# First attention loads inside the last slot of conv pass one, and value products of 512 columns in two pieces

## The chip, the cores and the metric

One core of a Trainium2 chip runs the whole program. The metric is the device time of one execution in microseconds; lower is better.

The engines are named as in the profile: PE (TensorE, matmuls and transposes; PEld is its weight load), DVE (VectorE), ACT (ScalarE), POOL (GpSimd), and SP (SyncE, which issues most DMAs).

## The reference, cut to what matters

One layer of a streaming encoder for 2048 prompt rows and 32 sample rows of width 1024. One input projection feeds a convolution branch (h, B, C, z) and an attention branch (q, k, v, z_att) of 8 heads of 64 channels:

```
xn = rmsnorm(x, norm_in)
h, bg, cg, zc, q, k, v, za = project_in(xn, w_in)       # 8 x 512 columns
yc = bg * short_conv(cg * h, conv_w) * silu(zc)
ya = band_attention(q, k, v, rel, valid, rel_bias) * silu(za)
x  = x + concat(rmsnorm(yc, norm_conv), rmsnorm(ya, norm_att)) @ w_out
x  = x + sigmoid(rmsnorm(x, ple_norm) @ w_ple_gate) * (p @ w_ple_proj)
y  = rmsnorm(x, final_norm)
```

The newest keys and values and the last convolution rows are outputs too. `band_attention` lets each chunk of 64 queries see its own chunk and the 8 before it; the sample rows see 512 cached keys.

## The kernel before, in words

**Numbers.** Every product is taken in two parts: each operand is split into a high part in fp32r and a low part (the rest), and `products` (line 274) adds high x high, high x low and low x high, three matmuls per 128 rows of the contraction. With KT = 8 such steps a block of output takes 24 matmuls.

**Memory.** GR (fp32r) and GF (fp32) are two large tiles of SBUF, cut by hand into areas by offset. X, the normalized input, lies in GR for all five column chunks (`CHUNKS`: 256, 384, 512, 512 and 416 rows of tokens). Two weight sets `WS` (each a high and a low half of 8 x 256 columns) lie behind it, 4096 columns apart. Behind those is `O_SP`, 1536 free columns. The attention's areas lie over those of X: the keys `K` and values `V` over chunk 0 and the start of chunk 1, and the queries `Q` in two buffers, `O_Q = [9216, O_SP]`: group g uses buffer g % 2. Offset 9216 is the end of chunk 1. PSUM has eight banks; pass one takes banks 0 to 4 in turn (`psm`), and transposes banks 5 to 7.

**Order of the work.** The order of all instructions is written out by hand; each engine runs its own in that order, and semaphores hold an instruction until what it reads is written and what it overwrites is read. DMAs issued by SP leave in SP's order.

- Keys first (slots 0 and 1), while X is made. Then slots 2 to 7 (line 1021): two of queries (s = 2, 3), two of values (s = 4, 5), two of the attention's gate (s = 6, 7). A slot has 256 columns of weights, which `load_w` brings to RAW and `split_w` (ACT makes the high part, line 194, DVE the low part, line 195) splits into `WS[s % 2]`. In each slot the loop runs over the five chunks; behind chunk 1 it splits the weights of the next slot and loads those of the one after.
- `values` (line 341) works by tiles of 128 tokens: X is the stationary operand, the 256 weight columns (four heads) the moving one, so that a slot has 17 tiles of 24 matmuls of 256 columns. ACT copies the high part of a tile out of PSUM, DVE makes the low part, SP stores both to DRAM (`vd`, line 339). Tiles of the newest 512 rows and of the sample rows are also copied out plain (line 355) and stored as outputs.
- `background` (line 410) is called once per chunk: it splits two blocks of 128 x 512 of the later weights (ACT line 376, DVE 377), which SP stores to DRAM, and lets ACT issue the loads of the next two (line 371).
- Conv pass one (line 1130) computes the convolution branch for chunks 0 and 1 in eight slots u = 0 to 7, in pairs of (h, C) and (B, z). Each slot first stores its split weights to DRAM (`store_wc`), because passes two and three load them again (`load_wc`, line 1058, 2 MB). In the (B, z) slots the output of a chunk is made by DVE and POOL (line 1113) in one buffer T2, and stored by SP (line 1114). Behind u = 6 come the loads of the attention's biases, whose corners POOL masks (line 491).
- Behind pass one SP issues the first loads of the attention (lines 1144 to 1146): keys and queries of group 0, its values and gate, then keys and queries of group 1. A group is two heads by 256 queries. `load_kq` issues six DMAs (lines 447 and 454), `load_vz` two (lines 463 and 467).
- Then `dense` runs passes two and three of the convolution on PE (line 1096), and between its matmuls the attention is advanced piece by piece: scores (line 546), maximum on DVE, exponential on ACT, normalization on POOL (line 578), transposes (line 618), products with the values (line 664). The first scores are due after 3% of the dense columns.
- At the end the output projections run tile by tile.

Of the kernel before, what the change touches and what calls it, by code (L numbers as in the profile page):

```python
# [9 lines left out]
F32R = mybir.dt.float32r  # L10
AF = mybir.ActivationFunctionType
ALU = mybir.AluOpType
# [3 lines left out]
T = 2048  # L16
S = 32
# [4 lines left out]
KW = 512  # L22
# [4 lines left out]
KT = 8  # L27

C0 = T
S0 = T + KW  # L30
NKEY = T + KW + S
NKT = (NKEY + 127) // 128
CHUNKS = [(0, 256), (256, 384), (640, 512), (1152, 512), (1664, 416)]
NCH = len(CHUNKS)
# [4 lines left out]
O_WS = [2 * KT * TT, 2 * KT * TT + 4096]  # L39
O_SP = O_WS[1] + 4096  # L40
# [5 lines left out]
O_K = [0, 1536]  # L46
O_V = 3072
O_PT = [6144, 7680]
O_Q = [9216, O_SP]
O_Z = [O_SP + 1024, O_SP + 1280]  # L50

O_WO = XO[2]
# [11 lines left out]
def hybrid_encoder_kernel(  # L64
# [6 lines left out]
    act, dve, pool, pe, sp = nc.scalar, nc.vector, nc.gpsimd, nc.tensor, nc.sync  # L71
# [5 lines left out]
    vp = v_prompt[0, 0].rearrange("t h d -> t (h d)")  # L77
    ks = k_sample[0, 0].rearrange("t h d -> t (h d)")
    vs = v_sample[0, 0].rearrange("t h d -> t (h d)")
# [7 lines left out]
    vd = tc.dram_tile((NKT * 128, H, 2, HD), F32, name="vd")  # L87
# [18 lines left out]
    PS = pspool.tile([128, 8, 512], F32, name="PS")  # L106

    def R(off, *shape):
        n = 1
        for s in shape:  # L110
            n *= s
        v = GR[:, off:off + n]
        return v if len(shape) == 1 else v.rearrange("p (a b) -> p a b", a=shape[0])

    def G(off, *shape):
        n = 1
        for s in shape:
            n *= s
        v = GF[:, off:off + n]
        return v if len(shape) == 1 else v.rearrange("p (a b) -> p a b", a=shape[0])  # L120
# [27 lines left out]
    Xh = [R(XO[c], KT, n) for c, (_, n) in enumerate(CHUNKS)]  # L148
    Xl = [R(XO[c] + KT * n, KT, n) for c, (_, n) in enumerate(CHUNKS)]
# [13 lines left out]
    psm = Ring([0, 1, 2, 3, 4])  # L163
    pst = Ring([5, 6, 7])

    def cols(kind, i):
        return DC * "hBCzqkva".index(kind) + 128 * i
# [8 lines left out]
    def load_w(s):  # L176
        if s >= NS:
            return
        (k0, i0), (k1, i1) = slots[s]
        if k0 == k1:  # L180
            c = cols(k0, i0)
            sp.dma_start(RAW, win[:, c:c + 256].rearrange("(k p) n -> p k n", p=128))
        else:
            for j, (kk, ii) in enumerate(slots[s]):
                c = cols(kk, ii)
                sp.dma_start(RAW[:, :, j * 128:(j + 1) * 128],
                             win[:, c:c + 128].rearrange("(k p) n -> p k n", p=128))

    def split_w(s, ks_=range(KT)):
        if s >= NS:  # L190
            return
        wh, wl = WS[s % 2]
        for k in ks_:
            act.activation(wh[:, k], RAW[:, k], AF.Copy, scale=cT[:, k:k + 1])  # L194
            dve.scalar_tensor_tensor(wl[:, k], RAW[:, k], cT[:, k:k + 1],  # L195
                                     wh[:, k].bitcast(F32), ALU.mult, ALU.subtract)
# [77 lines left out]
    def products(out, wh, wl, xh, xl, ks_=range(KT), mid=None):  # L274

        for k in ks_:
            if mid and k == KT // 2:
                mid()
            pe.matmul(out, wh(k), xh(k), start=(k == ks_[0]), stop=False)  # L279
            pe.matmul(out, wh(k), xl(k), start=False, stop=False)  # L280
            pe.matmul(out, wl(k), xh(k), start=False, stop=(k == ks_[-1]))  # L281

    def block(s, j, c, bank=None, mid=None):
        wh, wl = WS[s % 2]
        ps = PS[:, psm() if bank is None else bank, 0:CHUNKS[c][1]]
        js = slice(j * 128, (j + 1) * 128)
        products(ps, lambda k: wh[:, k, js], lambda k: wl[:, k, js],
                 lambda k: Xh[c][:, k, :], lambda k: Xl[c][:, k, :], mid=mid)
        return ps
# [43 lines left out]
    def split_v(dst_r, src, rows, r0, h0):  # L333
        vhl = vhl_r().rearrange("p (h a d) -> p h a d", h=4, a=2)
        p4 = src.rearrange("p (h d) -> p h d", h=4)
        act.activation(vhl[rows, :, 0, :].bitcast(F32R), p4[rows], AF.Copy)
        dve.tensor_tensor(vhl[rows, :, 1, :].bitcast(F32R), p4[rows], vhl[rows, :, 0, :],
                          ALU.subtract)
        sp.dma_start(vd[r0:r0 + rows.stop - rows.start, h0:h0 + 4], vhl[rows])

    def values(s, c):
        wh, wl = WS[s % 2]
        h0 = 4 * (slots[s][0][1] // 2)
        t0, n = CHUNKS[c]
        for o in list(range(0, n - 127, 128)) + ([n - 128] if n % 128 else []):
            ps = PS[:, psm(), 0:256]
            products(ps, lambda k: Xh[c][:, k, o:o + 128], lambda k: Xl[c][:, k, o:o + 128],
                     lambda k: wh[:, k, :], lambda k: wl[:, k, :])
            p0 = 0 if o % 128 == 0 else 128 - S
            r0 = t0 + o if not p0 else S0  # L350
            rows = slice(p0, 128)
            split_v(None, ps, rows, r0, h0)
            if r0 >= T - KW:
                VR = VR_r()
                act.activation(VR[rows], ps[rows], AF.Copy)
                dst = vs if p0 else vp[r0 - (T - KW):r0 - (T - KW) + 128]
                sp.dma_start(dst[:, h0 * HD:(h0 + 4) * HD], VR[rows])
# [52 lines left out]
    def background():  # L410

        for work, LW in loaded:
            work(LW)
        del loaded[:]
        while todo and len(loaded) < 2:
            load, work = todo.pop(0)
            LW = LW_r()
            load(LW)
            loaded.append((work, LW))
# [18 lines left out]
    def load_kq(g):  # L438

        if g >= len(groups):  # L440
            return
        p, m = groups[g]
        t0, kn, qn = (256 * m, 256, 256) if m < 8 else (T, KW + S, S)
        k0 = t0 % (RING * 128)
        for h in range(2):
            rows = slice((2 * p + h) * HD, (2 * p + h + 1) * HD)
            sp.dma_start(K[h][:, k0:k0 + kn].bitcast(F32),
                         kd[:, rows, t0:t0 + kn].rearrange("b c t -> c b t"))
            for b in range(2):
                q = Q[g % 2][h][b]  # L450
                if m == 8:
                    pool.memset(q[:, 0:2 * S].bitcast(F32), 0.0)
                    q = q[:, h * S:(h + 1) * S]
                sp.dma_start(q[:, 0:qn].bitcast(F32),
                             qs[b, rows, t0:t0 + qn].unsqueeze(1).to_broadcast([HD, 2, qn]))

    def load_vz(g):
        if g >= len(groups):
            return
        p, m = groups[g]  # L460
        m0, m1 = (2 * m, 2 * m + 2) if m < 8 else (16, NKT)
        v0 = m0 % RING
        sp.dma_start(
            V[:, v0:v0 + m1 - m0, :].bitcast(F32),
            vd[m0 * 128:m1 * 128, 2 * p:2 * p + 2].rearrange("(m t) h a d -> t m (h a d)", t=128))
        t0, qn = 256 * m, 256 if m < 8 else S
        sp.dma_start(Z[g % 2][:, 0:qn], zd[p * 128:(p + 1) * 128, t0:t0 + qn])
# [537 lines left out]
    def spread(h):  # L1005
        sp.dma_start(ext2[h], ext[h].unsqueeze(0).to_broadcast([128, 768]))
# [13 lines left out]
    NP1 = 8  # L1020
    for s in range(2, NP1):
        kind = slots[s][0][0]
        for c, (t0, n) in enumerate(CHUNKS):
            if 3 <= s < 7 and c < 2:
                spread(2 * (s - 3) + c)
            if kind == "v":
                values(s, c)
            else:
                p0 = block(s, 0, c)
                p1 = block(s, 1, c)  # L1030
            if kind == "q":
                release()
                for j, ps in enumerate((p0, p1)):
                    split_store(ps, qs, slots[s][j][1], [(0, n, t0)], -0.125)
            elif kind == "a":
                for j, ps in enumerate((p0, p1)):
                    i = slots[s][j][1]
                    za = za_r()
                    act.activation(za[:, :n], ps, AF.Silu)
                    sp.dma_start(zd[i * 128:(i + 1) * 128, t0:t0 + n], za[:, :n])  # L1040
            if c == 1:
                split_w(s + 1)
                load_w(s + 2)
            background()
# [85 lines left out]
    for u in range(8):  # L1130
        s = NP1 + u
        store_wc(s)
        for i, _ in enumerate(conv(u, psm)):
            if i == KT:
                split_w(s + 1)
                load_w(s + 2)
        if u >= 6:
            load_wc(u + 2)
        if u == 6:
            load_bias(0)  # L1140
            load_bias8(0)
            mask_bias(0)

    load_kq(0)
    load_vz(0)
    load_kq(1)
    banks = Ring([6, 7])

# [74 lines left out]
```

## Time and profile before

| what | value |
|---|---|
| median of 3 runs | 1450.62 us (1447.92 to 1453.04) |
| profiled execution | 1452.03 us, span 1450.1 us |
| PE busy | 1421.2 us, 98% of the span |
| ACT, DVE, POOL busy | 542.3, 607.8, 317.4 us |
| mean granted PE clock | 0.993 |
| DMA | 249.10 MB, mean 172 GB/s |

The span runs from the first to the last instruction of the profiled execution. Busy times of PE are pipelined: a matmul's listed duration overlaps the next one's, so the pace is read from the starts of successive matmuls, not from durations. A wait is listed under the instruction that waited, with what released it. The chain of waits is followed back from the last instruction, and shows what each step waited for last.

### The profile page before, as it was taken

The numbers are of one execution on the slowest core, as the hardware profiler recorded it, in microseconds if no ns is written. First come the engines' busy times: TensorE is split into PE (matmuls) and PEld (weight loads), VectorE is DVE, ScalarE is ACT, GpSimd is POOL, SyncE is SP. The second block draws the span as 40 slices with busy tenths as digits, with TensorE's granted clock in tenths as the row PEclk, the third lists the DMA queues.
The fourth block names the chain that finished last, engine by engine and source line by source line (L and its number), as shares of the span: only waits on it lengthen the run. The fifth ranks groups of instructions, "written<-read, shape, count | busy, mean of one in ns | idle before, by whom it ended". The sixth has DMA issues, their size and how long they took to land.

```text
span 1450.1 us, 22728 instructions
## 1 busy us (share of the span) xinstructions
PE 1421.2 (98%) x8362; PEld 1270.3 (88%) x8362; DVE 607.8 (42%) x1346; ACT 542.3 (37%) x1182; POOL 317.4 (22%) x438
## 2 busy tenths in 40 slices
PE   8999999999999989999999999999999999999997
PEld 8889989998899968888888989997788888888786
DVE  6323233321033416656656656663324233242333
ACT  7434233332132215545545545551123232232323
POOL 3310000000000013323323232332123332233322
PEclk9999999999999989999999999999999999999999
DMA  6526898885267564545555447767912212121200
GB/s 224 198 105 186 299 310 312 291 290 174 79 215 260 208 223 157 175 130 180 171 174 198 153 137 259 282 241 253 364 50 80 62 63 80 47 81 40 65 21 33
DMA packets 176391, 249.10 MB, mean 172 GB/s; under 512 B 19564, under 2 KB 124816, under 8 KB 170136
## 3 DMA queue, kind: packets, MB, share of 16 engines
q1 hardware_dynamic: 169712, 235.83, 48.0%
q10 hardware_dynamic: 6568, 11.82, 2.6%
q8 instruction: 66, 1.08, 0.3%
q14 instruction: 45, 0.37, 0.1%
HBM read 158.23 MB, written 92.50 MB: 173 GB/s over the span
## 4 chain that ended last, share of the span: by engine, by line
PE 90%; DMA 4%; issue 2%; DVE 2%; ACT 1%; POOL 1%; SPq 1%; POOLq 0%; ACTq 0%; DVEq 0%
PE PS L1096 22%; PE PS L279 17%; PE PS L280 17%; PE PS L281 17%; PE PS L546 5%; PE PS L664 4%; PE PS L618 3%; PE PS L662 1%; PE PS L869 1%; PE PS L827 1%; PE PS L268 1%; DMA GR<-wd 1%; DMA GF<-ext 1%; DVE GR L209 1%; DMA GR<-qs 0%
## 5 line engine op out<-in xcount | busy, mean ns | idle before, releaser
L279 PE MATMUL PS<-GR 128*128 128x512 f32 (+3 forms) x1336 | 476.4, 357 | 4.2 <-DVE GF L1126 1.7
L280 PE MATMUL PS<-GR 128*128 128x512 f32 (+3 forms) x1336 | 472.1, 353 | 1.2 <-DMA GR<-wd 0.7
L281 PE MATMUL PS<-GR 128*128 128x512 f32 (+3 forms) x1336 | 472.0, 353 | 0.5 <-DVE GR L810 0.5
L1096 PE MATMUL PS<-GR 128*128 128x512 f32 (+3 forms) x1920 | 423.0, 358 | 0.4 <-DMA GR<-wc 0.4
L1096 PEld LDWEIGHTS PS<-GR 128*128 128x128 f32 x1920 | 313.1, 190 | 17.9 <-DMA GR<-wc 0.8
L279 PEld LDWEIGHTS PS<-GR 128*128 128x128 f32 x1336 | 253.4, 190 | 35.6 <-DVE GF L1126 1.9
L281 PEld LDWEIGHTS PS<-GR 128*128 128x128 f32 x1336 | 253.4, 190 | 31.4 <-DVE GR L810 1.0
L280 PEld LDWEIGHTS PS<-GR 128*128 128x128 f32 x1336 | 253.6, 190 | 31.2 <-DMA GR<-wd 1.3
L578 POOL TENSOR_SCALAR GF<-GF,SM 128x640 f32<-128x640 f32 (+3 forms) x132 | 99.7, 756 | 243.7 <-DVE SM L572 178.3
L593 DVE TENSOR_TENSOR GR<-PS,GR 128x256 fp32r<-128x256 f32 (+2 forms) x184 | 97.6, 559 | 73.3 <-ACT GR L592 72.9
L1113 POOL TENSOR_TENSOR GF<-GF 128x512 f32<-128x512 f32 (+3 forms) x20 | 22.4, 1121 | 411.4 <-DVE GF L1112 400.6
L592 ACT ACTIVATE GR<-PS 128x256 fp32r<-128x256 f32 (+2 forms) x184 | 83.7, 491 | 75.5 <-PE PS L618 74.8
L558 DVE CUSTOM_DVE_ANT_0 GF<-PS,GF 128x640 f32<-128x640 f32 (+3 forms) x132 | 96.9, 734 | 28.4 <-PE PS L546 24.6
L566 ACT ACTIVATE GF<-GF,SM 128x640 f32<-128x640 f32 (+3 forms) x132 | 100.4, 761 | 16.6 <-DVE SM L558 15.8
L546 PE MATMUL PS<-GR 128*128 128x320 f32 (+6 forms) x512 | 93.1, 304 | 7.7 <-DMA GR<-qs 7.2
L908 DVE TENSOR_TENSOR GF<-PS,GF 128x512 f32<-128x512 f32 (+2 forms) x35 | 23.6, 675 | 176.2 <-ACT GF L907 176.2
L546 PEld LDWEIGHTS PS<-GR 128*128 128x128 f32 x512 | 82.4, 190 | 16.6 <-issue 7.6
L907 ACT ACTIVATE GF<-PS,SM 128x512 f32<-128x512 f32 (+2 forms) x35 | 23.6, 675 | 163.9 <-PE PS L281 82.7
L664 PE MATMUL PS<-GR 128*128 128x256 f32 x448 | 77.3, 289 | 0.0
L195 DVE SCALAR_TENSOR_TENSOR GR<-GF,cT,GR 128x256 fp32r<-128x256 f32 x112 | 45.8, 480 | 74.9 <-ACT GR L194 74.9
L910 POOL TENSOR_TENSOR GF<-GF 128x512 f32<-128x512 f32 (+1 forms) x32 | 41.1, 1286 | 159.6 <-DVE GF L908 141.5
L671 ACT ACTIVATE GF<-PS 64x256 f32<-64x256 f32 (+1 forms) x72 | 26.0, 361 | 125.7 <-PE PS L664 119.2
(139 smaller groups left out, 1343.6 us busy)
## 6 DMA issues: line engine op xcount, KB each, us to landing
GR<-wc SPq DMA_DIRECT2D x32, 1024.0 KB, 7.4
GR<-wd SPq DMA_DIRECT2D x72, 256.0 KB, 6.8
GF<-in_x_prompt_dram SPq DMA_DIRECT2D x32, 512.0 KB, 7.8
wc<-GR SPq DMA_DIRECT2D x16, 1024.0 KB, 7.5
GR<-qs SPq DMA_DIRECT2D x128, 128.0 KB, 3.0
wd<-GF SPq DMA_DIRECT2D x50, 256.0 KB, 5.9
GF<-in_w_in_dram SPq DMA_DIRECT2D x20, 512.0 KB, 6.0
vd<-GF SPq DMA_DIRECT2D x40, 256.0 KB, 4.5
```

What stands on the lines that cost most here:

```text
L195: dve.scalar_tensor_tensor(wl[:, k], RAW[:, k], cT[:, k:k + 1], wh[:, k].bitcast(F32), ALU.mult, ALU.subtract)
L279: pe.matmul(out, wh(k), xh(k), start=(k == ks_[0]), stop=False)
L280: pe.matmul(out, wh(k), xl(k), start=False, stop=False)
L281: pe.matmul(out, wl(k), xh(k), start=False, stop=(k == ks_[-1]))
L546: pe.matmul(ps[:, e, c:c + n_], q[h][b][:, qa], K[h][:, r:r + n_], start=(b == 0 and c == 0), stop=(b == 1), skip_group_check=True)
L558: dve.tensor_tensor_reduce(pr.rearrange("p (b c) -> p b c", b=nb), ps, br.rearrange("p (b c) -> p b c", b=nb), 1.0, 3e38, ALU.add, ALU.min ...
L566: act.activation(pr, pr, AF.Exp, bias=mx[rows], scale=-1.0, accum_out=sm[rows])
L578: pool.tensor_scalar(pr, pr, rs[rows], 1.0, ALU.mult, ALU.mult)
L592: act.activation(dst_of(hi), src, AF.Copy)
L593: dve.tensor_tensor(dst_of(lo), src, dst_of(hi).bitcast(F32), ALU.subtract)
L664: pe.matmul(PS[:, PS_AV, 0:256], v(k), t[:, slot_of[k], :], start=(i == 0), stop=(i == len(both) - 1))
L1096: pe.matmul(ps, a[:, k, js], b[c][:, k, :], start=(k == i == 0), stop=(k == KT - 1 and i == 2))
```

## The change

Three edits:

- `O_Q` is swapped: the queries of even groups, that of group 0 among them, lie at `O_SP`, those of odd groups at 9216.
- `load_kq(0)` and `load_vz(0)` move from behind pass one into its last slot (u = 7), behind the two blocks of chunk 0 (i = 2 KT - 1).
- In slot 4 the values of chunk 0 are made for that slot's four heads as before, and then `values_all` makes those of chunks 1 to 4 for all eight heads: the moving operand is 512 columns in two pieces of 256, one in each weight set, 4096 columns apart. Slot 5 is left with chunk 0 of its heads. The weights of slots 5 and 6 are split at the start of slots 4 and 5, the raw weights of slots 6 and 7 loaded there. A tile's evacuation, its store and its plain copy are each one instruction of 512 columns instead of two of 256; the plain copies have one buffer of 512 columns instead of two of 256. `background` is called 9 times in the two slots instead of 10.

```diff
-O_Q = [9216, O_SP]
+O_Q = [O_SP, 9216]
...
+    VW = [R(O_WS[0], 8192).rearrange("p (s b k n) -> p s b k n", s=2, b=2, k=KT)[:, :, b]
+          for b in range(2)]
+    VHL_r = Ring([G(6180, 1024), G(2084, 1024)])
+    VRW = G(3108, 512)
+
+    def values_all(c):
+        t0, n = CHUNKS[c]
+        for o in list(range(0, n - 127, 128)) + ([n - 128] if n % 128 else []):
+            bank = psm()
+            ps = PS[:, bank].rearrange("p (s n) -> p s n", s=2)
+            products(ps, lambda k: Xh[c][:, k, o:o + 128], lambda k: Xl[c][:, k, o:o + 128],
+                     lambda k: VW[0][:, :, k], lambda k: VW[1][:, :, k])
...
+            act.activation(vhl[rows, :, 0, :].bitcast(F32R), p8[rows], AF.Copy)
+            dve.tensor_tensor(vhl[rows, :, 1, :].bitcast(F32R), p8[rows], vhl[rows, :, 0, :],
+                              ALU.subtract)
+            sp.dma_start(vd[r0:r0 + 128 - p0], vhl[rows])
+            if r0 >= T - KW:
+                act.activation(VRW[rows], flat[rows], AF.Copy)
+                sp.dma_start(vs if p0 else vp[r0 - (T - KW):r0 - (T - KW) + 128], VRW[rows])
+            if o % 256 or p0:
+                background()
...
+        if kind == "v":
+
+            for h in range(2):
+                spread(2 * (s - 3) + h)
+            if s == 4:
+                split_w(5)
+                load_w(6)
+                values(4, 0)
+                background()
+                for c in range(1, NCH):
+                    values_all(c)
+            else:
+                split_w(6)
+                load_w(7)
+                values(5, 0)
+                background()
+            continue
...
+            if u == 7 and i == 2 * KT - 1:
+
+                load_kq(0)
+                load_vz(0)
...
-    load_kq(0)
-    load_vz(0)
     load_kq(1)
```

The line numbers of the changed kernel are larger: its store of the convolution output is L1157, its reload of weights L1101, key and query loads L476 and L483, values and gate L492 and L496, scores L575.

What SP issues around the end of pass one, before. `yd<-GF` are the two stores of slot u = 7 (chunk 0 with 256 columns, chunk 1 with 384), `GR<-wc` the reload of weights, `kd`, `qs`, `vd`, `zd` the DRAM copies of keys, queries, values and gate:

```order
L1052 DMA wc<-GR 128x2048 x2
L1114 DMA yd<-GF 128x256
L1114 DMA yd<-GF 128x384
L1058 DMA GR<-wc 128x2048 x2
L447 DMA GR<-kd 128x1x256
L454 DMA GR<-qs 128x1x256 x2
L447 DMA GR<-kd 128x1x256
L454 DMA GR<-qs 128x1x256 x2
L463 DMA GR<-vd 128x2x256
L467 DMA GR<-zd 128x256
```

And the same place now:

```order
L1095 DMA wc<-GR 128x2048 x2
L1157 DMA yd<-GF 128x256
L476 DMA GR<-kd 128x1x256
L483 DMA GR<-qs 128x1x256 x2
L476 DMA GR<-kd 128x1x256
L483 DMA GR<-qs 128x1x256 x2
L492 DMA GR<-vd 128x2x256
L496 DMA GR<-zd 128x256
L1157 DMA yd<-GF 128x384
L1101 DMA GR<-wc 128x2048 x2
L476 DMA GR<-kd 128x1x256
L483 DMA GR<-qs 128x1x256 x2
```

The eight loads of group 0 have moved ahead of chunk 1's store and of the reload; those of group 1 now follow the reload.

What ACT runs from the last tiles of slot 4 to the weight split of slot 6, before (L336 and L355 evacuate and copy out a tile, L376 and L371 are the background, L194 the split, here in slot 5 behind chunk 1):

```order
L336 ACTIVATE GF<-PS 32x4x64
L355 ACTIVATE GF<-PS 32x256
L376 ACTIVATE GR<-GF,cT 128x512
L376 ACTIVATE GF<-GF,cT 128x512
L371 DMA GF<-in_w_ple_gate_dram 128x512 x2
L336 ACTIVATE GF<-PS 128x4x64 x2
L376 ACTIVATE GF<-GF,cT 128x512
L376 ACTIVATE GR<-GF,cT 128x512
L371 DMA GF<-in_w_ple_gate_dram 128x512 x2
L336 ACTIVATE GF<-PS 128x4x64 x3
L194 ACTIVATE GR<-GF,cT 128x256 x8
```

And now (L360 and L365 evacuate and copy out a tile of 512 columns, L405 and L400 are the background, L336 evacuates a tile of slot 5):

```order
L360 ACTIVATE GF<-PS 32x8x64
L365 ACTIVATE GF<-PS 32x512
L405 ACTIVATE GR<-GF,cT 128x512
L405 ACTIVATE GF<-GF,cT 128x512
L400 DMA GF<-in_w_ple_gate_dram 128x512 x2
L194 ACTIVATE GR<-GF,cT 128x256 x8
L336 ACTIVATE GF<-PS 128x4x64 x2
```

The split of slot 6's weights stands directly behind the background of slot 4's last tile, ahead of both tiles that slot 5 still has.

More of the change, by code (lines that the diff above doesn't have):

```diff
@@ L339, in split_v @@
         sp.dma_start(vd[r0:r0 + rows.stop - rows.start, h0:h0 + 4], vhl[rows])
+    VW = [R(O_WS[0], 8192).rearrange("p (s b k n) -> p s b k n", s=2, b=2, k=KT)[:, :, b]
[9 more added lines that the diff above has]
+                     lambda k: VW[0][:, :, k], lambda k: VW[1][:, :, k])
+            p0 = 0 if o % 128 == 0 else 128 - S
+            r0 = t0 + o if not p0 else S0
+            rows = slice(p0, 128)
+            flat = PS[:, bank]
+            vhl = VHL_r().rearrange("p (h a d) -> p h a d", h=8, a=2)
+            p8 = flat.rearrange("p (h d) -> p h d", h=8)
+            act.activation(vhl[rows, :, 0, :].bitcast(F32R), p8[rows], AF.Copy)
[7 more added lines that the diff above has]
+                background()
     def values(s, c):
@@ L1025, in hybrid_encoder_kernel @@
                 spread(2 * (s - 3) + c)
[L1026 to L1030, printed above, removed]
+            p0 = block(s, 0, c)
+            p1 = block(s, 1, c)
             if kind == "q":
```

## The prediction

> **What bounds the kernel now.** I read the page first (span, engine shares, clock, chain), then the waits of TensorE (PE), then the chain of waits and the stretches around its longest wait, and last the timelines of PE and ScalarE (ACT) in the two slots that make the values.
>
> ```profile
> span 1450.1 us, 22728 instructions
> PE 1421.2 (98%) x8362; PEld 1270.3 (88%) x8362; DVE 607.8 (42%) x1346; ACT 542.3 (37%) x1182; POOL 317.4 (22%) x438
> PEclk9999999999999989999999999999999999999999
> PE 90%; DMA 4%; issue 2%; DVE 2%; ACT 1%; POOL 1%; SPq 1%; POOLq 0%; ACTq 0%; DVEq 0%
> ```
>
> PE is busy 98% of the span and the chain that ended last is 90% PE. So time is won only by fewer nanoseconds per matmul or by taking away one of the few waits of PE. The clock row has one digit below 9, the 15th of 40. PE's own waits, longest first:
>
> ```profile
> PE PS L546 <- DMA GR<-qs: 7.2, 1, 7.2
> PE PS L618 <- POOL GF L578: 2.0, 3, 0.7
> ```
>
> One wait of 7.2 us stands alone: the first score matmuls of the attention (L546) wait for the first queries. Every other line is 2.0 us or less. The chain around it, in order of time (start, length, what):
>
> ```profile
> 500.22 10.08 DMA GF<-ext
> ...
> 511.63 0.74 POOL GF L1113
> ...
> 512.39 4.38 DMA yd<-GF
> ...
> 517.37 0.56 DVE GF L1112
> ...
> 519.08 0.32 SPq L1114
> ...
> 520.43 0.60 SPq L447
> ...
> 521.08 7.14 DMA GR<-qs
> ...
> 528.36 0.73 PE PS L546 x2
> 529.09 3.95 PE PS L1096 x9
> ```
>
> The bias load lands at 510.3, Pool then masks it and makes the convolution output of chunk 0 (L1113), SP stores that at 512.39 and the output of chunk 1 at 519.08. Only then come the weights' reload (L1058, 2 MB) and, at 520.43, the first key load (L447); the queries behind it land 7.14 us after issue, behind the 2 MB. The stretches (start:end, length, busy us and instructions of PE, PEld, DVE, ACT, POOL, then granted clock, DMA share, GB/s):
>
> ```profile
> 513.60:521.10 7.50, 7.50 (x33) 5.84 (x32) 1.17 (x4) 2.37 (x3) 1.01 (x1) 1.00 0.33 92
> 521.10:528.30 7.20, 0.01 (x1) 0.00 (x0) 0.00 (x0) 0.00 (x0) 0.00 (x0) 0.72 0.95 364
> 528.30:534.50 6.20, 6.14 (x16) 5.06 (x17) 0.89 (x5) 1.03 (x4) 0.37 (x1) 0.50 0.85 259
> 534.70:537.10 2.40, 2.40 (x15) 2.01 (x14) 1.13 (x5) 0.50 (x2) 0.48 (x1) 1.00 0.72 216
> ```
>
> The wait costs more than its 7.2 us. The granted clock falls while PE idles and stays at 0.50 for 6.2 us of full work behind it: nine 512-column matmuls take 3.95 us, 0.44 us each.
>
> **The change, part by part.**
>
> *First loads.* SP now issues the keys, queries, values and gate of group 0 (eight DMAs) behind the store at 512.39 and ahead of the one at 519.08. Four things could hold them. (a) The buffers: keys and values lie over chunk 0 of X, which PE has read to the end before the store of 512.39 can be made from it; the queries of group 0 now lie over free space, since O_Q is swapped. Pool has no part in them (its memsets belong to m = 8). (b) SP itself, until 512.39. At about 0.6 us each, as L447 at 520.43, eight issues take until about 517.5, ahead of 519.08, so nothing behind them on SP is pushed back by more than a few tenths. (c) The transfers ahead of them: the store issued at 512.39 lands 4.38 us later, at 516.8. The page's issue table gives the ordinary landing of such a load:
>
> ```profile
> GR<-qs SPq DMA_DIRECT2D x128, 128.0 KB, 3.0
> ```
>
> The last query of head 0 is issued at about 514.6, so it lands at 517.6 undisturbed, and at about 518 to 519 if it comes out right behind the store. PE asks at 521.1. Two microseconds of margin. (d) DVE frees T2 and bank 0 of PSUM only after that store has landed; DVE is through at 517.9 (L1112), and 2 us later would still be ahead of 521.1. I take the whole wait as removed: 7.2 us. With it goes the half clock: 6.2 us at 0.50 is 3.1 us of lost pace. Together 10.3 us. If a wait of a few microseconds were left, only its difference to 7.2 would be won and perhaps none of the 3.1, so the bounds are 3 and 10.3. [...]
>
> What is late next is group 1, loaded behind the 2 MB reload in the place where group 0 was. Its queries should land where those of group 0 did, at 528.3. When does PE ask for them? The rows of PE from the first scores to the first of group 1 (L546 at 539.51):
>
> ```profile
> 528.88 4.15 PE L1096 MATMUL PS<-GR 128*128 128x512 f32 x9
> 533.26 2.16 PE L1096 MATMUL PS<-GR 128*128 128x512 f32 x6
> ...
> 535.42 1.61 PE L1096 MATMUL PS<-GR 128*128 128x512 f32 x6
> ...
> 537.10 0.85 PE L1096 MATMUL PS<-GR 128*128 128x512 f32 x3
> ...
> 538.03 1.64 PE L1096 MATMUL PS<-GR 128*128 128x512 f32 x6
> 539.51 0.51 PE L546 MATMUL PS<-GR 128*128 128x384 f32 x2
> ```
>
> That is 30 matmuls of 512 columns, 6.8 us at full clock (0.2264 each, below), and about 1.1 us of scores and transposes: 7.9 us. From 521.1 that is 529.0, against 528.3. The margin is 0.7 us, so I put 0.3 us for a wait there, bounds 0 and 2.
>
> *Values in 512 columns.* Chunks 1 to 4 hold 15 tiles of 128 tokens (the last is the 32 sample rows with 96 others). Each took 24 matmuls of 256 columns in each of two slots, 720 in all; now 24 of 512, 360 in all. Chunk 0 keeps its 2 x 48. The pace by start times, first and last of 48 matmuls of 256 columns (47 steps), then two starts 25 steps apart at 512 columns:
>
> ```profile
> 213.35 0.28 PE L279 MATMUL PS<-GR 128*128 128x256 f32 x1
> ...
> 218.98 0.28 PE L281 MATMUL PS<-GR 128*128 128x256 f32 x1
> ```
>
> ```profile
> 198.67 0.39 PE L281 MATMUL PS<-GR 128*128 128x512 f32 x1
> ...
> 204.33 0.35 PE L279 MATMUL PS<-GR 128*128 128x416 f32 x1
> ```
>
> 5.63 / 47 = 0.1198 us and 5.66 / 25 = 0.2264 us. So 720 x 0.1198 = 86.3 us becomes 360 x 0.2264 = 81.5 us: 4.8 us less. All of it is PE time on the path. Per matmul, whatever its length, about 13 ns lie beside the columns; halving the number halves those. [...] No row shows a moving operand in two pieces 16 KB apart. If the gap between the pieces costs as much as a new matmul, the saving is 0; I take no cost, since columns within each piece lie as in the 512-column rows.
>
> *The weight split moves next to its use.* Slot 5's weights are now split by ACT and DVE during the two chunk-0 tiles of slot 4, slot 6's during those of slot 5: 48 matmuls, 5.75 us, are all the cover, where before three chunks lay between. The rows: ACT's first free moment in slot 4; the last tile of slot 4 and the next tile; one split on ACT and on DVE; an evacuation of 512 columns on both:
>
> ```profile
> 217.28 0.38 ACT L336 ACTIVATE GF<-PS 128x256 fp32r<-128x256 f32 x1 [1.22 <-DVE GR L377]
> ...
> 262.39 0.38 ACT L336 ACTIVATE GF<-PS 32x256 fp32r<-32x256 f32 x1 [1.60 <-PE PS L281]
> ...
> 266.31 0.38 ACT L336 ACTIVATE GF<-PS 128x256 fp32r<-128x256 f32 x1 [1.30 <-DMA wd<-GR]
> ...
> 277.07 3.30 ACT L194 ACTIVATE GR<-GF,cT 128x256 fp32r<-128x256 f32 x8
> ```
>
> ```profile
> 277.61 3.28 DVE L195 SCALAR_TENSOR_TENSOR GR<-GF,cT,GR 128x256 fp32r<-128x256 f32 x8
> ```
>
> ```profile
> L294 ACT ACTIVATE GF<-PS 128x512 fp32r<-128x512 f32 x11 | 6.6, 597 | 25.8 <-PE PS L281 10.4 <-DMA wd<-GF 7.4 <-DMA kd<-GF 5.1
> L295 DVE SCALAR_TENSOR_TENSOR GF<-PS,GF 128x512 fp32r<-128x512 f32 x11 | 7.6, 691 | 33.3 <-ACT GF L294 28.1 <-DMA kd<-GF 5.2
> L337 DVE TENSOR_TENSOR GF<-PS,GF 128x256 fp32r<-128x256 f32 x32 | 13.4, 424 | 44.6 <-ACT GF L336 43.1 <-DMA wd<-GR 1.5
> ```
>
> Slot 4: ACT is free at 217.28, the first low part is ready 0.54 + 0.41 us later, at 218.2; PE wants it at 213.35 + 5.75 = 219.1. Covered. Slot 5: from the last tile's end to the next emission ACT needs 266.31 - 262.3 = 4.0 us (evacuate, wait for DVE, copy out, two background weight blocks, two load issues). With 512 columns the three evacuation steps grow by 0.21 + 0.27 + 0.21 us (597 ns against 0.38 us, 691 ns against 424), to 4.7 us. High parts follow from 5.1, low parts from 5.6 to 8.5 in steps of 0.41; PE asks for them from 6.0 to 8.5 in steps of 0.36. Just in time. Each microsecond that ACT is late becomes one of PE. The longest waits of ACT for a transfer in these slots were
>
> ```profile
> ACT GF L376 <- DMA GF<-in_w_out_dram: 3.3, 2, 2.0
> ```
>
> so I put 0.3 us, bounds 0 and 2. The single buffer VRW is one way to be late: its store leaves 2 us after a tile's end and must land within a further 5. The load of the next raw weights is issued right behind the split and holds SP until DVE has read the old ones; the stores of the values wait behind it, and with them the buffers of the next tiles. PE feels that only after its five banks are full, four tiles of 5.4 us (24 x 0.2264) later. The bank ring advances by 19 instead of 34, the same place modulo five.
>
> *The sum.* -10.3 - 4.8 + 0.3 + 0.3 = -14.5 us. The profiled execution took 1452.03 us for a span of 1450.1; it would take 1437.5. The median of the runs is 1450.62, 1.4 us below it, so I forecast 1436.1.
>
> **The rivals.**
>
> *The two pieces cost what a matmul costs.* Then the values save nothing and 1450.6 - 10.3 + 0.6 = 1440.9. For it: no row excludes it. Against it: none either but the even 0.2264 us of long streams. Chance 0.08.
>
> *The two pieces are slow (the slower side).* If the moving operand in two pieces were read at the pace of the half clock, 0.44 us for 512 columns, 360 matmuls would lose 360 x 0.21 = 77 us: 1450.6 + 77 - 9.7 = 1518. It decides from 15.1 / 360 = 42 ns per matmul. Against it: each piece is a contiguous run of 256 columns, as in the rows at 0.1198. [...] Chance 0.04.
>
> *The first loads are still late.* They share SP's queue with a store that needed 4.38 us and with the 2 MB of weights stored just ahead of it. If they land at 524, PE waits 3 us and may still lose part of the clock: 7.2 - 3 + 0 = 4.2 won here, 1450.6 - 4.2 - 4.8 + 0.3 = 1441.9. The same holds if group 1 comes 3 us late. Against it: a DMA share of 0.33 from 513.6 to 521.1. Chance 0.09.
>
> *The split of the weights is late.* DMA traffic in these slots runs at
>
> ```profile
> 219.10:311.20 92.10, 92.10 (x772) 92.10 (x771) 32.99 (x66) 33.82 (x75) 0.00 (x0) 1.00 0.87 305
> ```
>
> a share of 0.87, so a background block can arrive late, ACT waits with the split queued behind it, and PE stands. At 4 us this takes back most of the value term: 1440. Should PE idle long enough for the half clock, another 3 us go: 1443. Chance 0.07.
>
> **How the numbers follow.** The forecast has 0.72, the rivals 0.08, 0.04, 0.09 and 0.07. About 0.3%, 4.35 us, can be told from no change; all cases but the slow pieces (0.04) stay below 1446.3, and of the late loads I leave 0.05 for a loss large enough to fall within it. So faster 0.91, same 0.05, slower 0.04. Low end: no residual wait (15.1 us) and 2.5 us of run scatter (the three runs reach 2.7 below their median), 1433. High end: it takes in the rivals up to a late split with half clock, 1443.
>
> **What would show it.** Right: no wait of L575 (the score line's new number) on GR<-qs, clock 1.00 throughout that stretch, matmul starts 0.226 us apart in the 15 value tiles, and at most some tenths of a microsecond of wait where those tiles begin and where slot 6 begins. Wrong: starts of 0.24 us or more in those tiles; a clock digit of 8 about the 14th or 15th slice; PE waiting for L195 or L194 at the start of slot 6, or for GR<-qs about 8 us into the attention.

## The result, and the profile after

| what | before | after |
|---|---|---|
| median of 5 runs each | 1450.62 us (1447.92 to 1453.04) | 1436.60 us (1435.15 to 1438.36) |
| ratio, 95% interval | | 0.9905 (0.989 to 0.9919) |
| profiled execution, span | 1452.03, 1450.1 us | 1435.68, 1433.6 us |
| mean granted PE clock | 0.993 | 0.997 |

The kernel became 14.0 us faster; 14.5 had been forecast, against the median 1436.1 us. The page of the profile after, in the rows that answer to those of before (span, engine shares, clock row, chain):

```profile
span 1433.6 us, 21914 instructions
PE 1412.7 (99%) x8002; PEld 1248.0 (87%) x8002; DVE 605.1 (42%) x1331; ACT 538.4 (38%) x1162; POOL 316.6 (22%) x438
PEclk9999999999999999999999999999999999999999
PE 93%; DMA 2%; DVE 2%; ACT 1%; issue 1%; POOL 0%; SPq 0%; POOLq 0%; ACTq 0%; DVEq 0%
```

PE has 360 matmuls fewer, the 8 in the clock row is gone, and DMA's share of the chain that ended last fell from 4% to 2%. Of the waits of PE, here are the longest and one that is needed further down, for the cached keys early in the program (at 135.8 us; slot 4, where the change begins, starts at 212.9):

```profile
PE PS L647 <- POOL GF L607: 2.0, 3, 0.8
...
PE PS L418 <- DMA GF<-in_cache_k_dram: 0.6, 1, 0.6
```

The line that led this view before, 7.2 us for `GR<-qs`, is not there at all, in any size. The queue of SP shows why (start, time in SP's queue, instruction):

```profile
507.24 0.32 SPq L1157 DMA_DIRECT2D yd<-GF  x1
507.66 0.60 SPq L476 DMA_DIRECT2D GR<-kd  x1
508.31 1.24 SPq L483 DMA_DIRECT2D GR<-qs  x2
...
512.39 0.47 SPq L496 DMA_DIRECT2D GR<-zd  x1
513.91 0.32 SPq L1157 DMA_DIRECT2D yd<-GF  x1
514.33 1.86 SPq L1101 DMA_DIRECT2D GR<-wc  x2
```

The first keys and queries are issued between the two stores, and SP is through with all eight DMAs at 512.9, 1 us before the second store is ready. On PE the scores then follow the convolution without a gap (timeline of PE, start and length; the first row is the first scores, the last those of group 1):

```profile
516.69 0.33 PE L575 MATMUL PS<-GR 128*128 128x128 f32 x2
516.86 2.27 PE L1139 MATMUL PS<-GR 128*128 128x512 f32 x9
...
524.83 0.51 PE L575 MATMUL PS<-GR 128*128 128x384 f32 x2
```

No row ends in a bracket with a wait; nine matmuls of 512 columns take 2.10 us between the starts of their neighbours, where they took 3.95 us before. From the first scores to those of group 1 it is 8.14 us.

In the value tiles the pace is read from starts again: the first matmul of each of the first three tiles, of chunk 4's last tile, and of slot 5 behind it:

```profile
218.67 0.40 PE L279 MATMUL PS<-GR 128*128 128x512 f32 x1
...
224.14 0.39 PE L279 MATMUL PS<-GR 128*128 128x512 f32 x1
...
229.58 0.39 PE L279 MATMUL PS<-GR 128*128 128x512 f32 x1
...
295.23 0.39 PE L279 MATMUL PS<-GR 128*128 128x512 f32 x1
...
300.80 0.28 PE L279 MATMUL PS<-GR 128*128 128x256 f32 x1
```

The second tile takes 5.44 us for 24 matmuls, 0.2267 us each; the last takes 5.57, 0.232 each. All 360 take 82.13 us, 0.228 each. Before, with 256 columns, chunk 4's tiles were not slower than the others: its four tiles in slot 4 took 11.41 us for 96 matmuls (timeline of PE, the first start and the start behind the last), 0.119 us each where the other tiles took 0.120:

```profile
250.78 0.28 PE L279 MATMUL PS<-GR 128*128 128x256 f32 x1
...
262.19 0.28 PE L279 MATMUL PS<-GR 128*128 128x256 f32 x1
```

### The profile page after: what moved, and what is told of

It is laid out like the page before. It is cut to its first block, busy times and chain, and to the rows that moved or that the text cites. A ratio compares the mean times of both kernels' runs of the same rounds, so it can differ in the third digit from the quotient of the medians.

```text
span 1433.6 us, 21914 instructions
## 1 busy us (share of the span) xinstructions
PE 1412.7 (99%) x8002; PEld 1248.0 (87%) x8002; DVE 605.1 (42%) x1331; ACT 538.4 (38%) x1162; POOL 316.6 (22%) x438
## 4 chain that ended last, share of the span: by engine, by line
PE 93%; DMA 2%; DVE 2%; ACT 1%; issue 1%; POOL 0%; SPq 0%; POOLq 0%; ACTq 0%; DVEq 0%
PE PS L1139 25%; PE PS L279 17%; PE PS L281 17%; PE PS L280 17%; PE PS L575 5%; PE PS L693 4%; PE PS L647 3%; PE PS L691 1%; PE PS L898 1%; PE PS L856 1%; PE PS L268 1%; DMA GR<-wd 1%; DVE GR L209 1%; DMA out_dram<-GF 0%; PE PS L657 0%
## 5 line engine op out<-in xcount | busy, mean ns | idle before, releaser
L279 PE MATMUL PS<-GR 128*128 128x512 f32 (+3 forms) x1216 | 454.4, 374 | 4.4 <-DVE GF L1169 1.7
L280 PE MATMUL PS<-GR 128*128 128x512 f32 (+3 forms) x1216 | 450.1, 370 | 1.0 <-DVE GR L271 0.6
L281 PE MATMUL PS<-GR 128*128 128x512 f32 (+3 forms) x1216 | 450.3, 370 | 0.5 <-DVE GR L839 0.5
L1139 PE MATMUL PS<-GR 128*128 128x512 f32 (+3 forms) x1920 | 420.6, 357 | 0.0
L1139 PEld LDWEIGHTS PS<-GR 128*128 128x128 f32 x1920 | 311.2, 189 | 17.0 <-DMA GR<-wc 0.3
L279 PEld LDWEIGHTS PS<-GR 128*128 128x128 f32 x1216 | 229.3, 189 | 40.6 <-DVE GF L1169 1.9
L281 PEld LDWEIGHTS PS<-GR 128*128 128x128 f32 x1216 | 229.4, 189 | 36.3 <-DVE GR L839 1.0
L280 PEld LDWEIGHTS PS<-GR 128*128 128x128 f32 x1216 | 229.6, 189 | 35.7 <-DMA GR<-wd 1.1
L575 PE MATMUL PS<-GR 128*128 128x320 f32 (+6 forms) x512 | 92.5, 302 | 0.5 <-DVE SM L587 0.5
L575 PEld LDWEIGHTS PS<-GR 128*128 128x128 f32 x512 | 81.9, 188 | 9.0 <-DVE SM L587 1.2
L647 PE MATMUL PS<-ident,GF 128*128 128x128 f32 x448 | 69.1, 272 | 2.0 <-POOL GF L607 2.0
```

The lines of the kernel that those rows point to most:

```text
L575: pe.matmul(ps[:, e, c:c + n_], q[h][b][:, qa], K[h][:, r:r + n_], start=(b == 0 and c == 0), stop=(b == 1), skip_group_check=True)
L647: pe.transpose(ps[:, k - 1 - 2 * g, a * 128:(a + 1) * 128], got[a][0][:, b * 128:(b + 1) * 128], ident)
L1139: pe.matmul(ps, a[:, k, js], b[c][:, k, :], start=(k == i == 0), stop=(k == KT - 1 and i == 2))
```

## The experiments

The theory: the gain is three things that add up, the wait of the first scores, the half clock that this wait leaves behind, and the time per matmul that the longer value products save. The rivals: one part carries all of it, the two pieces cost something, or the wait only moves to another place. Times of single runs scatter by 2 or 3 us (the runs of before span 5 us), so those are read by their traces. They are set against the median of the changed kernel, 1436.60 us; its profiled execution, whose trace the waits are compared with, took 1435.68.

**One part at a time.** First the load move with the swap of `O_Q`, with values, their splits and `background` as before (the cut is against the changed kernel):

```diff
-        if kind == "v":
...
-                for c in range(1, NCH):
-                    values_all(c)
...
+            if kind == "v":
+                values(s, c)
+            else:
```

> Before with the swap of O_Q and the early loads of group 0 only; the values as before. Theory (the wait of 7.2 us and the half clock behind it, 3.1 us, are both gone): 10.3 us less than before, 1440.3, ratio 0.9929; no wait of the scores on GR<-qs, granted clock 1.00 behind them. Rival (the half clock has another cause and stays): 7.2 us less, 1443.4, ratio 0.9950, clock 0.50 for some 6 us. Rival (the value part carries more than its share): less than 7 us gained.

Measured: 1440.19 us (1439.47 to 1442.25, 6 runs) against 1449.98, ratio 0.993 (0.9912 to 0.9947). That is 9.8 us, between 7.7 and 12.8 by the interval, so the time alone barely excludes a gain of the 7.2 us wait only; the trace decides, in which the clock stays at 1.00 from the first scores on. The first scores do not wait. The scores of group 1 do, for a moment (timeline of PE, the bracket is the wait and its releaser):

```profile
528.98 0.70 PE L546 MATMUL PS<-GR 128*128 128x384 f32 x2 [0.87 <-DMA GR<-qs]
```

The clock stayed at 1.00 through this wait too. So group 1's place, predicted with a margin of 0.7 us, is on the edge: 0.9 us late here, not late in the trace of the changed kernel.

Then the values alone, with the loads behind pass one and `O_Q` as before:

```diff
-O_Q = [O_SP, 9216]
+O_Q = [9216, O_SP]
...
+    load_kq(0)
+    load_vz(0)
     load_kq(1)
```

> Before with the value products of chunks 1 to 4 in 512 columns only; the first loads as before. Theory: the 15 tiles at the pace seen in the changed kernel take 82.1 us instead of 86.2, and slot 6 starts 0.2 us late: 3.9 us less than before, 1446.7, ratio 0.9973; the wait of the scores on GR<-qs is back at 7.2 us, with the half clock. Rival (the two parts help each other): no more than 2 us gained.

Measured: 1446.24 us (1443.44 to 1448.15, 10 runs), ratio 0.9969 (0.9956 to 0.9981). The wait is back, at 6.1 us, and behind it the clock stays at 0.50 until 530.6 us, 5.4 us of work:

```profile
PE PS L575 <- DMA GR<-qs: 6.1, 1, 6.1
```

The parts give 9.8 and 3.7 us, 13.5 together, and both at once gave 14.0: they add within the scatter, and neither carries the other.

**Is the swap of `O_Q` needed?** The changed kernel with the old `O_Q` alone. The old buffer, columns 9216 to 10240 of GR, is the last third of the low half of X's chunk 1, so chunk 1's last slot finds the queries of group 0 in place of that part.

```diff
-O_Q = [O_SP, 9216]
+O_Q = [9216, O_SP]
```

> The changed kernel with O_Q as before: the queries of group 0 lie over the end of chunk 1 of X, so their load waits for the end of pass one. Theory: that end comes about 1 us after the issue in the changed kernel, 7.5 us ahead of the scores; the queries land about 4 us ahead, no wait, same time as the changed kernel within 1.5 us. Rival (the swap is what makes the early loads work): the scores wait 2 us or more.

Measured: 1447.42 us. There is a wait, but in another place than either the theory or the rival had it. The load is written ahead of chunk 1's last reads, so it is the matmuls of that chunk that wait for the load (the waits of PE):

```profile
PE PS L1139 <- DMA GR<-qs: 8.7, 2, 8.2
```

The first scores then don't wait at all. The 8.7 us and some 3 us from the half clock behind them are about what this single run lost. The order in which the overlapping accesses are written decided who waited, and here it was the engine that bounds the kernel. The swap is what lets the early load be free: without it 10.8 us of the 14.0 are gone in this run.

**How early must the loads be?** Group 0's loads behind the second store of pass one, still ahead of the 2 MB reload:

```diff
-            if u == 7 and i == 2 * KT - 1:
-                load_kq(0)
-                load_vz(0)
+        if u == 7:
+            load_kq(0)
+            load_vz(0)
         if u >= 6:
             load_wc(u + 2)
```

> The changed kernel with the loads of group 0 behind pass one's last store and ahead of the reload of weights (2 MB). They leave about 2.4 us before the scores and need 2.9 us to land after the last issue: PE waits about 2 us. Theory (the clock halves only behind a long wait): clock 1.00 behind it, time 2 us above the changed kernel, span near 1435.6. Rival (any wait of microseconds halves the clock): a stretch at 0.50 and another 2 to 3 us.

Measured: 1442.14 us, 5.5 us over the changed kernel, more than I expected. The first scores waited 1.0 and 0.4 us, where about 2 had been expected. What I had missed is the next in the queue, group 1, which is pushed back by the same issues (timeline of PE):

```profile
518.97 0.30 PE L575 MATMUL PS<-GR 128*128 128x128 f32 x1 [1.02 <-DMA GR<-qs]
519.65 0.33 PE L575 MATMUL PS<-GR 128*128 128x128 f32 x1 [0.38 <-DMA GR<-qs]
...
530.21 0.82 PE L575 MATMUL PS<-GR 128*128 128x384 f32 x2 [2.21 <-DMA GR<-qs]
```

and behind this second wait the clock halved for 3.4 us, shown below. The account: 1.02 + 0.38 + 2.21 us of waits and about 3.41 / 2 = 1.7 us of clock are 5.3 us. The wait for the cached keys is 1.9 us in this trace, 1.3 more than in that of the changed kernel; with it the parts come to 6.6 us, against 6.5 from profiled execution to profiled execution.

Then the same loads between the two halves of the reload, values and gate first, to make a wait between those two:

```diff
         for b, w in enumerate(WS[u % 2]):
             sp.dma_start(w.bitcast(F32).rearrange("p k n -> p (k n)"), wc[u % 8, b])
+            if u == 9 and b == 0:
+                load_vz(0)
+                load_kq(0)
...
-            if u == 7 and i == 2 * KT - 1:
-
-                load_kq(0)
-                load_vz(0)
```

> The changed kernel with the loads of group 0 between the two halves of the reload of weights, values and gate first, then keys and queries. By the times of the changed kernel the last query of head 0 is issued 1 us after the scores ask for it and lands behind 1 MB: PE waits about 4 us, between the 1.4 us that left the clock at 1.00 in the run with the loads ahead of the reload and the 6.1 us that halved it in the run with the values only. Theory (PE's thin stretch decides, some 2 to 3 us of it suffice): a stretch at 0.50, 6 to 7 us above the changed kernel, 1442.6 to 1443.6. Rival (only waits of 6 us or more halve the clock): the wait alone, 1440.6.

Measured: 1447.24 us, 10.6 us above the changed kernel, where 6 to 7 had been expected. PE waited 5.0 us:

```profile
524.34 0.74 PE L575 MATMUL PS<-GR 128*128 128x128 f32 x2 [5.02 <-DMA GR<-qs]
```

The clock was at 0.50 until 529.6 (stretches, the granted clock third from the end), so 5.3 us of work ran at about half pace:

```profile
526.19:529.60 3.41, 3.41 (x10) 2.75 (x9) 0.10 (x1) 0.00 (x0) 0.37 (x1) 0.50 1.01 359
529.60:533.01 3.41, 3.41 (x18) 2.86 (x17) 1.74 (x8) 1.10 (x4) 0.77 (x2) 1.00 0.86 266
```

Wait and clock give 5.0 + 2.6 = 7.6 us of the 10.6. Another 1.5 us is the wait for the cached keys (in PE's waits, against 0.6 in the changed kernel):

```profile
PE PS L418 <- DMA GF<-in_cache_k_dram: 2.1, 1, 2.1
```

1.5 us are left over. This trace (mean granted clock 0.994, the changed kernel's 0.997) has two more spells of half clock that the changed kernel's has not, at 137.1 us, behind the wait for the cached keys, and at 1014.3 us, 3.41 us each; the changed kernel's has one at 12.0 us that is missing here. One such spell is worth about what is left, some 1.6 us by the paces measured below. Behind this wait of 5.0 us the clock was at 0.50 too: the rival by which only 6 us and more halve it falls.

**Do the two pieces cost anything?** The moving operand as 512 neighbouring columns, the second half of which are other weights:

```diff
-    VW = [R(O_WS[0], 8192).rearrange("p (s b k n) -> p s b k n", s=2, b=2, k=KT)[:, :, b]
-          for b in range(2)]
+    VW = [[R(O_WS[0] + 2048 * b + 256 * k, 2, 256) for k in range(KT)] for b in range(2)]
...
-                     lambda k: VW[0][:, :, k], lambda k: VW[1][:, :, k])
+                     lambda k: VW[0][k], lambda k: VW[1][k])
```

> The changed kernel with the moving operand of the 15 value tiles in one piece: 512 neighbouring columns of the first weight set in place of 256 of each set (so the values of half the heads come from other columns; everything else is as before). Theory (two pieces cost nothing beside a few ns): the same starts, 0.2267 us apart, in the tiles of chunks 1 to 3; the 0.2321 us of chunk 4's tiles stays, since those tiles differ in the stationary operand. Rival (the gap between the pieces costs those 5 ns): 0.2267 or less in all 15 tiles, 0.5 us less in total.

Measured: 1439.59 us; of the 3.0 us above the changed kernel 1.6 are the wait for the cached keys (2.2 us here), and this trace too has the two further spells, at 136.3 and 1006.7 us. So the time says nothing of the pieces, but the tiles do. They have the same pace (timeline of PE: the starts of the first three tiles, and of slot 5 behind the last):

```profile
220.79 0.40 PE L279 MATMUL PS<-GR 128*128 128x512 f32 x1
...
226.26 0.39 PE L279 MATMUL PS<-GR 128*128 128x512 f32 x1
...
231.70 0.39 PE L279 MATMUL PS<-GR 128*128 128x512 f32 x1
...
302.92 0.28 PE L279 MATMUL PS<-GR 128*128 128x256 f32 x1
```

5.47 and 5.44 us for the first two tiles, and 302.92 - 220.79 = 82.13 us for all fifteen, as with two pieces to the last digit. Two pieces of 256 columns cost nothing here. Nor do they make chunk 4's four tiles slower (0.232 us per matmul in both); what does is not settled.

**What is behind the weight split's thin cover?** One more `background` in slot 5, ahead of the split:

```diff
             else:
+                background()
                 split_w(6)
```

> The changed kernel with one more pair of background blocks ahead of the weight split of slot 6: ACT waits for two loads it has just issued, splits them and issues two more, so the split starts about 6 us later. Theory (the split is just in time, and each microsecond of ACT becomes one of PE): PE waits about 6 us for the split where slot 6 begins, the clock halves behind it, 8 to 9 us above the changed kernel, 1445. Rival (work in between covers it): less than 1 us.

Measured: 1448.09 us. ACT waited 5.4 us for the extra weight blocks, and with the split queued behind them PE stood still (timelines of ACT and of PE):

```profile
311.62 0.72 ACT L405 ACTIVATE GF<-GF,cT 128x512 fp32r<-128x512 f32 x1 [5.40 <-DMA GF<-in_w_ple_gate_dram]
...
315.46 0.58 PE L279 MATMUL PS<-GR 128*128 128x256 f32 x1 [6.83 <-ACT GR L194]
```

Half clock followed until 321.7. Six matmuls of 256 columns lie between the two starts below, 0.213 us each where 0.120 is the pace at the full clock (timeline of PE; the last row is a stretch, with the granted clock third from the end):

```profile
317.00 0.41 PE L279 MATMUL PS<-GR 128*128 128x256 f32 x1
...
318.28 0.41 PE L279 MATMUL PS<-GR 128*128 128x256 f32 x1
...
319.00:321.00 2.00, 2.00 (x11) 2.00 (x11) 1.27 (x4) 1.22 (x2) 0.00 (x0) 0.50 0.64 162
```

At that pace 6.2 us of work lose 2.7 us. 6.8 + 2.7 = 9.5 us, and 1.4 of the wait for the cached keys, make 10.9 of the 11.5 us; the two further spells are in this trace too, at 137.4 and 1014.6 us. Wait and clock were put at 8 to 9 us. The theory has it right that ACT's lateness goes to PE as a wait. What the time has above it is in part a longer wait and in part not this experiment's doing.

**Can group 1's edge be taken away too?** Its keys and queries ahead of the reload as well:

```diff
+        if u == 7:
+            load_kq(1)
         if u >= 6:
             load_wc(u + 2)
...
-    load_kq(1)
```

> The changed kernel with keys and queries of group 1 also ahead of the reload of weights. Theory: they land some 5 us before their scores instead of within a microsecond of them; the wait of 0.9 us that the run with the loads only showed there cannot come, and the reload, 2 us later, is still 10 us early: 0 to 0.9 us less than the changed kernel, 1436.2, within what can be told from it. Rival (the reload becomes late): PE waits for GR<-wc at the next slot, 2 us slower.

Measured: 1435.64 us (1433.45 to 1438.26, 4 runs), ratio 0.9889 (0.9873 to 0.9906). No score matmul waits for its first loads, and the scores of group 1 come 8.14 us behind the first, as in the changed kernel. The interval overlaps that of the changed kernel (0.989 to 0.9919), so it is no faster that can be told. PE's waits hold none for `GR<-wc`, so the rival, a late reload, falls. Whether it takes away the risk of the 0.9 us is not shown by one trace, since that of the changed kernel had no such wait either.

## Why the prediction was right

- **The wait, -7.2 us.** Gone whole. The steps on SP's queue came out as worked: SP through with the eight issues before the second store, the first scores on time. The values-only kernel and the loads amid the reload show that the place of these loads alone brings it back.
- **The half clock, -3.1 us.** Right in size. From the first scores to those of group 1 it was 11.15 us before and is 8.14 now, 3.0 less. At a granted clock of 0.50, matmuls of 512 columns start 0.427 us apart (before, from 1019.58 us on) against 0.227, not quite twice; by that 6.2 us lose 2.9. The loads alone gave 9.8 us, with 0.9 us of wait left in its trace, where 7.2 + 3.1 - 0.3 = 10.0 had been put.
- **Group 1, +0.3 us.** The distance between the first scores and group 1's was put at 7.9 us and was 8.14. The wait was 0 in the changed kernel and 0.9 in the loads-only kernel, inside the bounds of 0 and 2.
- **The values, -4.8 us.** This term was too large by 0.7 us: the 360 matmuls took 82.1 us and not 81.5, and the 720 before them 86.2 and not 86.3, so 4.1 us were saved. Eleven tiles went at the predicted pace (0.2267 against 0.2264, the first tile 0.2279); chunk 4's four, at 0.232, make up 0.5 us. The prediction took its pace from other 512-column rows, none of which had chunk 4's rows of X as the stationary operand. Those rows alone are not it, since with 256 columns their tiles were no slower than the others; the cause stays open, and the sign that had been named, 0.226 us in all 15 tiles, held in eleven.
- **The split, +0.3 us.** This too came as worked. In ACT's timeline the last tile's evacuation, the copy and two weight blocks stand ahead of the split:

```profile
301.00 0.59 ACT L360 ACTIVATE GF<-PS 32x512 fp32r<-32x512 f32 x1 [3.62 <-PE PS L281]
302.36 0.59 ACT L365 ACTIVATE GF<-PS 32x512 f32<-32x512 f32 x1 [0.76 <-DVE GF L361]
...
305.56 3.31 ACT L194 ACTIVATE GR<-GF,cT 128x256 fp32r<-128x256 f32 x8 [1.25 <-DVE GF L406]
```

It begins 4.7 us behind the tile's end at 300.9, the number predicted. PE meets it in slot 6's first block, where every third matmul, the one with the low part, takes 0.04 to 0.05 us longer:

```profile
307.90 0.32 PE L281 MATMUL PS<-GR 128*128 128x256 f32 x1
308.06 0.28 PE L279 MATMUL PS<-GR 128*128 128x256 f32 x1
308.18 0.28 PE L280 MATMUL PS<-GR 128*128 128x256 f32 x1
308.29 0.33 PE L281 MATMUL PS<-GR 128*128 128x256 f32 x1
```

From one L281 to the next it is 0.39 to 0.41 us where 0.36 is the pace: PE follows DVE's steps of 0.41 (eight in 3.29 us). Over the block that is 0.22 us (24 matmuls in 3.10 us against 2.88).

By landmarks of the two traces the values and the split gave 3.8 us (from the start of slot 4 to the second block of slot 6), the wait 7.2 and the stretch from the first scores to group 1's 3.0, 14.1 in all with the further digits. So of the 14.5 us that were forecast, 0.7 too much on the values and 0.1 on the clock stand against 0.3 charged for a wait of group 1 that did not come and 0.1 too much charged for the split: the misses cancel in part.

The two spans differ by 16.5: another 0.4 is a wait for `GR<-wc`, 0.4 the wait for the cached keys (1.0 us before), and some 1.6 lie in a spell of half clock at the start of the output stage, which before's trace has and after's hasn't, in code that the change doesn't touch. That spell does not go with the change: the traces of the loads amid the reload, the one piece, the late split and group 1 ahead of the reload have it, between 1004.7 and 1014.6 us, and those of the other four experiments haven't. What decides it is not shown. The runs behind the median differ in clock too: of the five of the changed kernel the longest, 1438.36 us, has a mean granted clock of 0.995, the others 0.997. So that the medians differ by 14.0, as the landmarks do, is partly chance.

Of the rivals, the cost of two pieces fell with the kernel of one piece, in its free form and in the slow one: with the moving operand as two runs of 256 columns and as one of 512, a matmul of the second tile takes 0.2267 us. The late loads and the late split are real, 5.5 and 10.6 us and 11.5 us above the changed kernel when forced, but the kernel keeps clear of the first, and touches the second by 0.2 us.

## What to carry to other kernels

A wait of the bounding engine is priced with what follows it: the one of 7.2 us cost 10.2. When a load is moved up in a queue, ask who is behind it (a second place in that queue became late by 2.2 us), and where it lands: without the swap the early load, written ahead of the last reads of its area, made PE wait 8.7 us. A work step that is moved next to its use should be timed with every instruction ahead of it on its engine; a margin of nothing cost 0.2 us here while all was on time, and about 9.5 when ACT was held up 5.4 us by a transfer.

## What the runs showed of the hardware

The spells of half clock in these traces are not of any length: they begin and end on a grid of 3.41 us. Here is before's trace cut at the moments where the clock changes (start:end, length, busy of PE, PEld, DVE, ACT, POOL, granted clock, DMA share, GB/s):

```profile
520.92:524.33 3.41, 0.20 (x1) 0.00 (x0) 0.00 (x0) 0.15 (x1) 0.00 (x0) 1.00 0.83 315
524.33:527.74 3.41, 0.00 (x0) 0.00 (x0) 0.00 (x0) 0.00 (x0) 0.00 (x0) 0.50 1.01 395
527.74:531.16 3.42, 2.80 (x8) 2.35 (x9) 0.46 (x3) 0.50 (x2) 0.37 (x1) 0.50 1.02 327
531.16:534.57 3.41, 3.41 (x11) 2.73 (x10) 0.43 (x2) 0.60 (x2) 0.00 (x0) 0.50 0.73 211
534.57:537.98 3.41, 3.41 (x19) 2.84 (x18) 1.66 (x7) 0.50 (x2) 0.85 (x2) 1.00 0.60 180
...
1015.85:1019.26 3.41, 2.04 (x6) 1.01 (x7) 0.00 (x0) 0.00 (x0) 0.00 (x0) 1.00 1.02 303
1019.26:1022.67 3.41, 3.41 (x10) 2.65 (x9) 0.75 (x1) 0.00 (x0) 0.00 (x0) 0.50 0.96 303
1022.67:1026.08 3.41, 3.41 (x18) 2.76 (x17) 1.73 (x3) 2.01 (x2) 1.17 (x1) 1.00 1.05 385
```

Each row is one step of the grid. In these rows the clock goes with the row above: the steps with 0.20 us and with none of busy PE are followed by 0.50, and the two at 0.50 that PE works through, 3.41 us busy, by 1.00. The step with 0.6 us of wait in it (527.74) did not yet bring it back. How much of a wait is too much is not sharp by these figures: a step with 2.90 us of busy PE was followed by 1.00 (the changed kernel's, from 12.01), one with 2.96 by 0.50 (without the swap, from 512.17). The second spell lies on the same grid: from 524.33 to 1019.26 are 494.93 us, 145 steps of 3.413. The kernel with the loads ahead of the reload shows the same on its own grid:

```profile
517.43:520.84 3.41, 2.02 (x10) 1.29 (x9) 0.30 (x2) 0.98 (x3) 0.00 (x0) 1.00 0.66 188
520.84:524.25 3.41, 3.41 (x18) 2.87 (x17) 1.23 (x5) 0.61 (x3) 0.80 (x2) 1.00 0.72 216
...
527.67:531.08 3.41, 1.21 (x7) 0.68 (x6) 0.09 (x1) 0.00 (x0) 0.48 (x1) 1.00 1.02 361
531.08:534.49 3.41, 3.41 (x12) 2.77 (x11) 1.15 (x4) 0.98 (x3) 0.60 (x1) 0.50 0.96 297
```

Behind 1.4 us of waits in one step the clock stayed at 1.00, behind 2.2 us in another it was 0.50, and it fell 0.9 us after PE was back at work. In before's trace a step with 2.04 us of busy PE was followed by half clock, here one with 2.02 was not, so the busy time that the profile gives does not tell the two apart. In the whole traces of before and of the changed kernel, and in the steps around the long waits of the experiments, steps at full clock with at most 1.2 us of busy PE were followed by half clock and those with 2.3 or more by full clock. Between them there are both: full clock behind 1.70 (the changed kernel's, from 991.64), 1.71 (before's, from 1005.61) and the 2.02 above, half clock behind 1.82 (before's, from 8.92), 1.99 (the changed kernel's, from 8.60) and the 2.04. Behind the first 20 us and ahead of the end of PE's work, the spells in the traces are one step (before at 1019, this one, and those near 137 us in three of the experiments and near 1010 us in four), two (6.8 us: the values alone, and the loads amid the reload) and three (10.2 us: before's long wait, the kernel without the swap, the late split). So what the five long waits, of 5.0 to 8.7 us, left behind them was a started step and a whole one at half clock. From these steps and the paces below, that makes an estimate of 3.4 to 6.8 us of work, or some 1.6 to 3.2 us of time; it was 6.2 us of work behind the 7.2 us wait, 5.4 behind the 6.1, 5.3 behind the 5.0 and 6.2 behind the late split's 6.8. In these rows half clock is not quite half the pace: 0.427 against 0.227 us for 512 columns and 0.213 against 0.120 for 256, 1.9 and 1.8 times.
